# Two 256-token blocks per PSUM bank and eviction, HGRN products on VectorE, norm factors ahead of weight splits

## Chip, core and metric

One core of one Trainium2 chip runs the whole program. The metric is the device time of one execution in microseconds (us); lower is better.

## What is computed

Sequence 256, model width 1024, float32 in and out. A first block (a mixer of four branches, then a SwiGLU feed-forward, then a norm) is followed by a second block of two layers: an HGRN2 mixer and a feed-forward, an RG-LRU mixer and a feed-forward, and a last norm. Cut to what the change touches:

```python
# HGRN2, 8 heads of 128: S_t = diag(f_t) S_{t-1} + (1-f_t) i_t^T, o_t = S_t^T q_t
q, fl, v, g = split(rmsnorm(x, norm_mix_2[0]) @ hgrn_w_in)      # 4 x 1024 columns
lb = cumsum(softmax(hgrn_lb, axis=0), axis=0)[0]                # the floor of f
q = silu(q); f = lb + (1 - lb) * sigmoid(fl); k = (1 - lb) * sigmoid(-fl)
o = rmsnorm_per_head(recurrence(q, k, f, v)) * hgrn_norm * silu(g)
x = x + o @ hgrn_w_out
# RG-LRU
y, u = split(rmsnorm(x, norm_mix_2[1]) @ lru_w_in)              # 2 x 1024 columns
uc = causal_conv4(u); r = sigmoid(uc @ wa + ba); i = sigmoid(uc @ wx + bx)
a = exp(-8 * r * softplus(-lam)); b = sqrt(1 - a*a) * (i * uc)
x = x + (linear_scan(a, b) * gelu(y)) @ lru_w_out
```

## The kernel before

Every float32 product is made of three matmuls on split operands: `hh`, `hl` are the high and low part of the normed input, `whi`, `wlo` those of a weight. A weight unit `raw` (1 MB) comes by DMA on SP's queue into one of four buffers and is split in two halves of 128x1024: `whi` is a copy on ACT, `wlo` a subtraction on DVE (`split`, L99 and L100; with `burst` set, four of them on POOL). There are four buffers of each half.

Two forms of projection exist. `gemm_a` gives tokens on partitions, matmuls of 512 columns. `gemm_b` gives features on partitions: a block of 128 features by 256 tokens, eight k steps of three 256-column matmuls, 24 matmuls (`block_b`, L153 to L155). The pool of accumulators `acc` has four PSUM banks, one for each block. An eviction multiplies the block by `rrow`, the row of the norm's factors 1/rms, which `make_row` makes on PE from two diagonal tiles `dg` and ACT copies (L265); so matmuls may start before the factor is known, evictions may not. The factor itself is `rstd`: a sum, a scaling (L235, L241) and a power on POOL (L245).

Users of `gemm_b`: the first mixer's convolution inputs (`xin`) and query/key blocks (`qk`), HGRN's q and f blocks (`u`, L778 and L785), the LRU's convolution inputs (`xin`, L929) and its y blocks (`yg`, L977). In HGRN, POOL multiplies `hq = u * sigmoid(u)` (L781), makes the pair products `pr` and their low part `pl` (L833, L835), and scales the residual `x` by the factor `rf` of the first block's last norm (L1098). HGRN's scores are then built in seven levels (`tp` tiles of L864, with `hq`, `hk` multiplied by `G` in between, L868, L869, and `st` filled by L871), with HGRN's v and g projections (`acc`, 512 columns) as PE work between the levels. Each head group ends in an out chain: state products `tp<-hv,st` (L894), squares (L899, ACT), a factor (L241, L245), two multiplications to `on` (L902, L904), PE transposes of `on` (L273), a split into `oh` and `ol`, the output projection.

Instructions of each engine run in the order that a scheduler wrote at build time, by dependencies and priorities; weight splits have priority offset 400.

Of the kernel before, what the change touches and what calls it, by code (L numbers as in the profile page):

```python
# [74 lines left out]
class Build:  # L75
    def __init__(self, tc, a):
        self.tc, self.nc, self.a = tc, tc.nc, a
        self.uid = 0
        self.turn = 0
        self.share = 0  # L80
        self.parts = 2
        self.hold = []
        self.burst = 0
        self.wmore = None
        self.place = -1

# [144 lines left out]
    def rstd(self, ss, scale=1.0 / D):  # L231
# [3 lines left out]
        nc.vector.tensor_tensor(r, ss[:, :, 0], ss[:, :, 1], op=ALU.add)  # L235
        self.rsqrt(r, r, scale)
# [20 lines left out]
    def make_row(self, r):  # L257
        nc = self.nc
# [113 lines left out]
    def mixer(self, hk, r, rr, x, finish):  # L372
        nc, a, tc = self.nc, self.a, self.tc
        w_in = a["w_in"][0]
        with tc.tile_pool(name="yT", bufs=3) as ytp, tc.tile_pool(name="att", bufs=1) as at, \
# [136 lines left out]
            for ps in self.gemm_b(hk, w_in, 5136, 1):  # L512
                nc.vector.tensor_tensor(kd, ps, rr(), op=ALU.mult)
# [54 lines left out]

    def lru_rates(self):
# [21 lines left out]
    def conv_inputs(self, pool, n):  # L591

        xins = [pool.tile([P, S + 3], F32, name=self.nm("xin")) for _ in range(n)]
        for xin in xins:
            self.nc.vector.memset(xin[:, 0:3], 0.0)
        return xins
# [8 lines left out]
    def mamba(self, hk, r, rr, w_in, mp, rows4, dtc, acol, yT, then):  # L605
# [4 lines left out]
        xins = self.conv_inputs(mp, 2)  # L610
        for b in (4, 6, 0, 2):
            for j, ps in enumerate(self.gemm_b(hk, w_in, 512 + b * P, 2)):
                blk = b + j
                xin = xins[j]
                nc.vector.tensor_tensor(xin[:, 3:], ps, rr(), op=ALU.mult)
# [131 lines left out]
    def hgrn(self, hk, r, rr, x, finish):  # L747
# [3 lines left out]
        w = a["hgrn_w_in_2"][0]  # L751
        LV = (64, 32, 16, 8, 4, 2, 1)
        with tc.tile_pool(name="hgrn", bufs=1) as hp:
            lbp = self.col["hgrn_lb_2"]
            lb = hp.tile([P, 8], F32, name="lb")
            om = hp.tile([P, 8], F32, name="om")
            lt = hp.tile([P, 2, 8], F32, name="lt")
            nc.vector.tensor_tensor(lb, lbp[:, 0:8], lbp[:, 8:16], op=ALU.max)
            for i in range(2):
                nc.vector.tensor_tensor(lt[:, i], lbp[:, i * 8:(i + 1) * 8], lb, op=ALU.subtract)  # L760
            nc.scalar.activation(lt, lt, AF.Exp)
            nc.vector.tensor_tensor(om, lt[:, 0], lt[:, 1], op=ALU.add)
            nc.vector.reciprocal(om, om)
            nc.vector.tensor_tensor(lb, lt[:, 0], om, op=ALU.mult)
            nc.vector.tensor_tensor(om, lt[:, 1], om, op=ALU.mult)
# [58 lines left out]
    def hgrn_scores(self, hp, q, k, f, masks, LV):  # L824
# [83 lines left out]
    def lru(self, hk, r, rr, x, finish):  # L908
        nc, a, tc = self.nc, self.a, self.tc
        w = a["lru_w_in_2"][0]  # L910
        with tc.tile_pool(name="lru", bufs=1) as lp:
# [10 lines left out]
            xins = self.conv_inputs(lp, 4)  # L922

            def conv(n):
                g, m = divmod(n, 2)
                for i, ps in enumerate(self.gemm_b(hk, w, D + n * 256, 2)):
                    b = 2 * n + i
                    xin = xins[b % 4]
                    nc.vector.tensor_tensor(xin[:, 3:], ps, rr(), op=ALU.mult)  # L929
                    self.conv4(uc[g][:, 2 * m + i], xin, [cw[:, k * 8 + b:k * 8 + b + 1] for k in range(4)],  # L930
# [228 lines left out]
```

## Time and profile before

| | |
|---|---|
| median of 3 runs | 1181.28 us (1181.03 to 1183.28) |
| the profiled execution | 1183.03 us, of which 1181.3 us span and 1.7 us around it |
| PE / DVE / ACT / POOL busy | 96% / 62% / 52% / 7% of the span |
| mean granted TensorE clock | 0.987 |

A row of a timeline gives start, duration, engine, source line, operation, output<-inputs, shapes, count, and in brackets the engine's idle time before it and what ended that.

### The profile page before, as it was taken

The numbers are of one execution on the slowest core, as the hardware profiler recorded it, in microseconds if no ns is written. First come the engines' busy times: TensorE is split into PE (matmuls) and PEld (weight loads), VectorE is DVE, ScalarE is ACT, GpSimd is POOL, SyncE is SP. The second block draws the span as 40 slices with busy tenths as digits, with TensorE's granted clock in tenths as the row PEclk, the third lists the DMA queues.
The fourth block names the chain that finished last, engine by engine and source line by source line (L and its number), as shares of the span: only waits on it lengthen the run. The fifth ranks groups of instructions, "written<-read, shape, count | busy, mean of one in ns | idle before, by whom it ended". The sixth has DMA issues, their size and how long they took to land.

```text
span 1181.3 us, 15772 instructions
## 1 busy us (share of the span) xinstructions
PE 1139.4 (96%) x6308; PEld 980.3 (83%) x6308; DVE 737.3 (62%) x971; ACT 615.4 (52%) x908; POOL 82.9 (7%) x87
## 2 busy tenths in 40 slices
PE   7999999999999999998999999999998789999997
PEld 7899897888888888888989878888888778888886
DVE  7876655565575555456998575555556776555552
ACT  7655656754555445346543465444446775445441
POOL 1100010000000000007510140000000000000000
PEclk9999999999999999999999999999998889999999
DMA  9795345455556555555443347555554546555540
GB/s 298 192 283 169 87 156 181 149 178 180 202 178 195 190 178 179 184 180 171 142 145 108 106 143 250 181 183 168 200 159 147 175 126 203 188 178 178 163 159 36
DMA packets 120761, 202.78 MB, mean 172 GB/s; under 512 B 4244, under 2 KB 44437, under 8 KB 120688
## 3 DMA queue, kind: packets, MB, share of 16 engines
q1 hardware_dynamic: 117264, 192.59, 49.8%
q0 software_dynamic: 2992, 8.56, 2.6%
q8 instruction: 49, 0.80, 0.3%
q10 hardware_dynamic: 432, 0.63, 0.2%
q14 instruction: 24, 0.20, 0.0%
HBM read 200.64 MB, written 4.25 MB: 173 GB/s over the span
## 4 chain that ended last, share of the span: by engine, by line
PE 86%; DVE 6%; ACT 4%; DMA 3%; issue 2%; POOLq 0%; POOL 0%; ACTq 0%; DVEq 0%
PE acc L154 26%; PE acc L155 26%; PE acc L153 26%; DVE wlo L100 2%; DMA raw<-in_w_in_dram 2%; PE tp L273 2%; PE tp L864 2%; PE tp L694 1%; ACT whi L99 1%; PE tp L207 1%; PE tp L723 1%; DVE uc L603 0%; PE tp L731 0%; DMA rows<-acd 0%; DVE G L875 0%
## 5 line engine op out<-in xcount | busy, mean ns | idle before, releaser
L100 DVE TENSOR_TENSOR wlo<-raw,whi 128x1024 fp32r<-128x1024 f32 (+3 forms) x364 | 442.2, 1220 | 310.0 <-ACT whi L99 303.3
L99 ACT CAST whi<-raw 128x1024 fp32r<-128x1024 f32 (+3 forms) x372 | 382.1, 1033 | 365.4 <-PE acc L155 299.7
L155 PE MATMUL acc<-whi,hl 128*128 128x512 f32 (+2 forms) x832 | 316.3, 381 | 0.0
L154 PE MATMUL acc<-wlo,hh 128*128 128x512 f32 (+2 forms) x832 | 313.6, 377 | 1.3 <-DVE wlo L100 1.3
L153 PE MATMUL acc<-whi,hh 128*128 128x512 f32 (+2 forms) x832 | 311.3, 378 | 1.4 <-ACT whi L99 1.1
L154 PEld LDWEIGHTS acc<-wlo,hh 128*128 128x128 f32 x832 | 156.4, 188 | 31.1 <-DVE wlo L100 2.4
L153 PEld LDWEIGHTS acc<-whi,hh 128*128 128x128 f32 x832 | 156.3, 188 | 28.7 <-ACT whi L99 2.0
L155 PEld LDWEIGHTS acc<-whi,hl 128*128 128x128 f32 x832 | 156.4, 188 | 28.1 <-issue 0.7
L153 PE MATMUL acc<-hh,whi 128*128 128x256 f32 (+1 forms) x496 | 140.2, 285 | 5.7 <-DVE u L778 2.7
L155 PE MATMUL acc<-hh,wlo 128*128 128x256 f32 (+1 forms) x496 | 140.0, 284 | 1.4 <-DVE wlo L100 1.4
L154 PE MATMUL acc<-hl,whi 128*128 128x256 f32 (+1 forms) x496 | 140.2, 284 | 0.4 <-DVE hl L100 0.4
L154 PE MATMUL acc<-wlo,ah 128*128 128x512 f32 x264 | 103.1, 391 | 0.0
L155 PE MATMUL acc<-whi,al 128*128 128x512 f32 x264 | 102.6, 389 | 0.0
L153 PE MATMUL acc<-whi,ah 128*128 128x512 f32 x264 | 102.5, 390 | 0.0
L153 PEld LDWEIGHTS acc<-hh,whi 128*128 128x128 f32 (+1 forms) x496 | 93.5, 190 | 8.6 <-ACT whi L99 3.6
L155 PEld LDWEIGHTS acc<-hh,wlo 128*128 128x128 f32 (+1 forms) x496 | 93.7, 189 | 2.4 <-DVE wlo L100 2.2
L154 PEld LDWEIGHTS acc<-hl,whi 128*128 128x128 f32 (+1 forms) x496 | 94.1, 190 | 1.4 <-DVE hl L100 0.6
L155 PEld LDWEIGHTS acc<-whi,al 128*128 128x128 f32 x264 | 49.6, 188 | 10.2
L153 PEld LDWEIGHTS acc<-whi,ah 128*128 128x128 f32 x264 | 49.5, 188 | 10.2
L154 PEld LDWEIGHTS acc<-wlo,ah 128*128 128x128 f32 x264 | 49.6, 188 | 10.0
L99 ACT CAST ah<-tp 128x512 fp32r<-128x512 f32 (+1 forms) x36 | 19.8, 551 | 34.0 <-PE tp L273 34.0
L329 ACT ACTIVATE sg<-acc,rstd 128x512 f32<-128x512 f32 (+1 forms) x36 | 23.3, 648 | 20.4 <-PE acc L155 20.4
(306 smaller groups left out, 1260.0 us busy)
## 6 DMA issues: line engine op xcount, KB each, us to landing
raw<-in_ffn_w_in_dram SPq DMA_DIRECT2D x44, 1024.0 KB, 5.2
raw<-in_w_in_dram SPq DMA_DIRECT2D x33, 1024.0 KB, 5.2
raw<-in_ffn_w_out_dram SPq DMA_DIRECT2D x20, 1024.0 KB, 5.1
raw<-in_hgrn_w_in_dram SPq DMA_DIRECT2D x16, 1024.0 KB, 5.4
raw<-in_w_ffn_gate_dram SPq DMA_DIRECT2D x11, 1024.0 KB, 5.1
raw<-in_w_ffn_up_dram SPq DMA_DIRECT2D x11, 1024.0 KB, 5.1
raw<-in_w_ffn_down_dram SPq DMA_DIRECT2D x10, 1024.0 KB, 5.1
raw<-in_w_branch_dram SPq DMA_DIRECT2D x8, 1024.0 KB, 5.1
```

Source lines behind the costliest of these rows:

```text
L99: self.nc.scalar.copy(hi, src)
L100: (eng or self.nc.vector).tensor_tensor(lo, src, hi.bitcast(F32), op=ALU.subtract)
L153: mm(ps, sh, mh, start=start, stop=False)
L154: mm(ps, sh, ml, start=False, stop=False)
L155: mm(ps, sl, mh, start=False, stop=stop)
L207: last = nc.tensor.transpose(ps[:, j * P:(j + 1) * P], xc[:, j * P:(j + 1) * P], self.ident)
L273: nc.tensor.transpose(ps[:, j * P:(j + 1) * P], src[:, j * P:(j + 1) * P], self.ident)
L329: nc.scalar.activation(sg[:, :n], psg[t][:, :n], AF.Silu, scale=r[:, t:t + 1])
L694: nc.tensor.matmul(ps[par][:, jj * W:(jj + 1) * W], qT[pr, 2 * gi + jj, qt * P:(qt + 1) * P], kT(2 * gi + jj)[pr, :W], start=True, stop=True)
L723: nc.tensor.transpose(ps[:, i * P:(i + 1) * P], sp[:, i, b * P:(b + 1) * P], self.ident)
L864: nc.tensor.matmul(ps[:, c:c + 64], k[:, h, ts], q[:, h, ts].rearrange("p (n u l) -> p n u l", u=2, l=L)[:, :, 1], start=True, stop=True)
```

## The change

`gemm_b` puts the two blocks of a pair into the two halves of one bank, with k outermost and the blocks inside it, and hands back one 128x2x256 view; `times_row` evicts it in one instruction. The four banks hold four pairs. Users are rewritten to pairs (`xin`, `qk`, `u`, `sgq`, `yg`; `u` has two buffers of a pair, `sgq` one). HGRN's `hq`, `pr` and `pl` are made on DVE, its `x*rf` on ACT. The floors `lb`, `om` are made by a function called beside the first feed-forward (the scheduler puts them in front of the program's first matmuls). `rstd`, the row and the chain of `rf` get priority offset 600.

```diff
     def gemm_b(self, hk, w, c0, nblk):
         wk = self.wunit(w, 0, 8, c0, nblk * P)
-        return [self.block_b(hk, wk, slice(b * P, (b + 1) * P)) for b in range(nblk)]
+        ps = self.acc()
+        n, mm = len(hk), self.nc.tensor.matmul
+        with self.held():
+            for k, (h, l) in enumerate(hk):
+                for b in range(nblk):
+                    o, (wh, wl) = ps[:, b * S:(b + 1) * S], (u[:, b * P:(b + 1) * P] for u in wk[k])
+                    mm(o, wh, h, start=k == 0 and b == 0, stop=False, skip_group_check=True)
+                    mm(o, wh, l, start=False, stop=False, skip_group_check=True)
+                    mm(o, wl, h, start=False, stop=k == n - 1, skip_group_check=True)
+        return ps[:, :nblk * S].rearrange("p (b s) -> p b s", s=S)
+
+    def times_row(self, out, ps, rr):
+        self.nc.vector.tensor_tensor(out, ps, rr.unsqueeze(1).to_broadcast([P, ps.shape[1], S]), op=ALU.mult)
...
         r = self.small.tile([P, 2], F32, tag="rstd", name=self.nm("rstd"))
-        nc.vector.tensor_tensor(r, ss[:, :, 0], ss[:, :, 1], op=ALU.add)
-        self.rsqrt(r, r, scale)
+        with self.tc.high_priority(offset=self.rush):
+            nc.vector.tensor_tensor(r, ss[:, :, 0], ss[:, :, 1], op=ALU.add)
+            self.rsqrt(r, r, scale)
...
-                    for i, ps in enumerate(self.gemm_b(hk, w, h0 * P, 2)):
-                        u = hp.tile([P, S], F32, tag="u", name=self.nm("u"), bufs=3)
-                        nc.vector.tensor_tensor(u, ps, rr(), op=ALU.mult)
-                        sg = hp.tile([P, S], F32, tag="sgq", name=self.nm("sgq"), bufs=2)
-                        nc.scalar.activation(sg, u, AF.Sigmoid)
-                        nc.gpsimd.tensor_tensor(q[:, 2 * c + i], u, sg, op=ALU.mult)
...
+                    u = hp.tile([P, 2, S], F32, tag="u", name=self.nm("u"), bufs=2)
+                    self.times_row(u, ps, rr())
+                    sg = hp.tile([P, 2, S], F32, tag="sgq", name=self.nm("sgq"), bufs=1)
+                    nc.scalar.activation(sg, u, AF.Sigmoid)
+                    nc.vector.tensor_tensor(q[:, hs], u, sg, op=ALU.mult)
...
+            for t in range(2):
+                nc.scalar.activation(x[:, t], x[:, t], AF.Copy, scale=rf[:, t:t + 1])
...
-        nc.gpsimd.tensor_tensor(pr, q.rearrange("p h t -> p (h t)"), k.rearrange("p h t -> p (h t)"), op=ALU.mult)
-        nc.scalar.copy(ph, pr)
-        nc.gpsimd.tensor_tensor(pl, pr, ph.bitcast(F32), op=ALU.subtract)
+        nc.vector.tensor_tensor(pr, q.rearrange("p h t -> p (h t)"), k.rearrange("p h t -> p (h t)"), op=ALU.mult)
+        self.split(ph, pl, pr)
...
-            for t in range(2):
-                nc.gpsimd.tensor_scalar(x[:, t], x[:, t], rf[:, t:t + 1], None, op0=ALU.mult)
```

Source lines shift: of the lines above, the evictions are L202 after, `split` L100 and L101, the matmuls of pairs L195 to L197, the row L282 to L285, the transposes of `on` L293, the state products L919, `x*rf` L816.

The first place is the start of HGRN on DVE. Before, the floors stand between the factor's steps (L1090 to L1093 are `rstd`, L762 to L765 the floors), and each block has its own eviction:

```order
L1091 TENSOR_TENSOR rstd_4717<-rstd_4717,rf_4720 128x2
L762 TENSOR_TENSOR om<-lt 128x8
L1092 TENSOR_SCALAR rstd_4717<-rstd_4717 128x2
L763 RECIPROCAL om<-om 128x8
L1093 TENSOR_TENSOR rstd_4717<-rstd_4717,rf 128x2
L764 TENSOR_TENSOR lb<-lt,om 128x8
L765 TENSOR_TENSOR om<-lt,om 128x8
L100 TENSOR_TENSOR wlo_4982<-raw_4979,whi_4981 128x1024
L262 TENSOR_SCALAR dg_4820<-ident,rstd_4717 128x128
L262 TENSOR_SCALAR dg_4823<-ident,rstd_4717 128x128
L100 TENSOR_TENSOR wlo_4986<-raw_4979,whi_4985 128x1024
L778 TENSOR_TENSOR u_4818<-acc_4768,rrow_4826 128x256
```

The same place on DVE in the changed program:

```order
L1116 TENSOR_TENSOR rstd_4702<-rstd_4702,rf_4705 128x2
L1117 TENSOR_SCALAR rstd_4702<-rstd_4702 128x2
L1118 TENSOR_TENSOR rstd_4702<-rstd_4702,rf 128x2
L282 TENSOR_SCALAR dg_4791<-ident,rstd_4702 128x128
L282 TENSOR_SCALAR dg_4794<-ident,rstd_4702 128x128
L101 TENSOR_TENSOR wlo_4937<-raw_4934,whi_4936 128x1024
L202 TENSOR_TENSOR u_4789<-acc_4740,rrow_4797 128x512
L202 TENSOR_TENSOR u_4862<-acc_4813,rrow_4797 128x512
L101 TENSOR_TENSOR wlo_4941<-raw_4934,whi_4940 128x1024
L101 TENSOR_TENSOR wlo_5007<-raw_5004,whi_5006 128x1024
L805 TENSOR_TENSOR hq_4727<-u_4789,sgq_4800 128x512
```

The floors and a weight split are gone from in front of `dg`; the evictions are pairs; `hq` has joined the queue. On ACT the same stretch now has the residual's scaling ahead of a weight half and of the row:

```order
L1101 ACTIVATE junk_4697,ss_3278<-x 128x512
L816 ACTIVATE x<-x,rf 128x1024 x2
L100 CAST whi_4936<-raw_4934 128x1024
L285 COPY rrow_4797<-tp_4790 128x256
L100 CAST whi_4940<-raw_4934 128x1024
```

Before, an exponential with its table load stood there, and POOL held the scaling.

The second place is HGRN's first out chain on PE. Before, the last score products (L880), the state products (L894) and the transposes of `on` (L273) have 24 matmuls of HGRN's last projection between the last two (12 for `acc_5872` and 12 for `acc_5873`, of which the first and the last rows):

```order
L880 MATMUL tp_5597<-hq_5051,hk_5052 128x128 x4
L894 MATMUL tp_5750<-hv,st_5366 128x128 x4
L153 MATMUL acc_5872<-whi_5910,hh_3296 128x512
L154 MATMUL acc_5872<-wlo_5911,hh_3296 128x512
...
L154 MATMUL acc_5873<-wlo_5915,hh_3296 128x512
L155 MATMUL acc_5873<-whi_5914,hl_3298 128x512
L273 MATMUL tp_5766<-ident,on_5763 128x128 x4
```

In the changed program that projection is finished earlier, and PE has:

```order
L889 MATMUL tp_5508<-hq_5001,hk_5002 128x64 x8
L155 MATMUL acc_5803<-wlo_5845,hh_3270 128x512
L156 MATMUL acc_5803<-whi_5844,hl_3272 128x512
L905 MATMUL tp_5520<-hq_4727,hk_4728 128x128 x4
L905 MATMUL tp_5527<-hq_5001,hk_5002 128x128 x4
L919 MATMUL tp_5680<-hv,st_5296 128x128 x4
L293 MATMUL tp_5696<-ident,on_5693 128x128 x4
```

Nothing stands between the state products and the transposes any more; 43 matmuls of the v and g projections have moved ahead of the score levels.

The third place is the start of the LRU on DVE. Before, four blocks are evicted one behind the other, ahead of the convolution taps (L603):

```order
L100 TENSOR_TENSOR wlo_7917<-raw_7910,whi_7916 128x1024
L929 TENSOR_TENSOR xin_7605<-acc_7623,rrow_7680 128x256
L929 TENSOR_TENSOR xin_7606<-acc_7648,rrow_7680 128x256
L929 TENSOR_TENSOR xin_7607<-acc_7706,rrow_7680 128x256
L929 TENSOR_TENSOR xin_7608<-acc_7731,rrow_7680 128x256
L603 SCALAR_TENSOR_TENSOR uc_7597<-xin_7605,pcol,uc_7597 128x256 x2
```

The same place after:

```order
L101 TENSOR_TENSOR wlo_7928<-raw_7921,whi_7927 128x1024
L202 TENSOR_TENSOR xin_7535<-acc_7549,rrow_7605 128x2x256
L101 TENSOR_TENSOR wlo_7837<-raw_7830,whi_7836 128x1024
L636 SCALAR_TENSOR_TENSOR uc_7527<-xin_7535,pcol,uc_7527 128x256 x2
L202 TENSOR_TENSOR xin_7536<-acc_7630,rrow_7605 128x2x256
```

Taps now start behind the first pair, and PE's order has the second half of three pairs (`acc_7549`, `acc_7630`, then `acc_7702` of the y blocks, 23 matmuls each) one behind the other, where before the four `xin` blocks were finished first and 48 matmuls of y blocks followed.

## Rows read from the trace of the kernel before

**Rows 1.** The page: busy time of two engines, and the shares of the chain that ended last.

```profile
PE 1139.4 (96%) x6308; PEld 980.3 (83%) x6308; DVE 737.3 (62%) x971; ACT 615.4 (52%) x908; POOL 82.9 (7%) x87
PE 86%; DVE 6%; ACT 4%; DMA 3%; issue 2%; POOLq 0%; POOL 0%; ACTq 0%; DVEq 0%
```

**Rows 2.** The view of waits, PE: what it waited for, us in total, times, longest.

```profile
PE acc L153 <- ACT uh L99: 6.7, 2, 4.4
PE acc L153 <- ACT loh L99: 5.9, 1, 5.9
...
PE acc L153 <- DVE u L778: 2.7, 1, 2.7
PE tp L653 <- DVE mt L651: 1.6, 1, 1.6
PE acc L155 <- DVE wlo L100: 1.4, 2, 1.1
...
PE acc L155 <- DVE ol L104: 1.1, 2, 0.7
...
PE acc L154 <- DVE hl L100: 0.4, 1, 0.4
...
PE acc L153 <- DVE xin L615: 0.3, 1, 0.3
```

**Rows 3.** Windows of PE alone: stretch, its length, PE busy (and matmuls), granted clock, DMA share, GB/s. The first follows the wait for `u`, the second the wait for `loh`, the third is a feed-forward.

```profile
552.90:560.00 7.10, 7.08 (x47) 0.76 0.47 148
962.80:968.00 5.20, 5.14 (x15) 0.64 0.46 133
700.00:860.00 160.00, 160.00 (x777) 1.00 0.59 194
```

**Rows 4.** PE's timeline: a 512-column matmul that waited for a weight half.

```profile
603.64 0.50 PE L154 MATMUL acc<-wlo,hh 128*128 128x512 f32 x1 [0.75 <-DVE wlo L100]
```

**Rows 5.** A window of HGRN from the first eviction to the end of the first score level: length, then busy us and instructions of PE, weight loads, DVE, ACT, POOL, then clock.

```profile
552.40:612.20 59.80, 56.91 (x388) 52.27 (x388) 53.11 (x76) 29.95 (x47) 28.84 (x28) 0.97 0.45 142
```

**Rows 6.** DVE's instructions of the same window by line: count, busy us, mean ns, idle before.

```profile
L100 DVE TENSOR_TENSOR wlo<-raw,whi 128x1024 fp32r<-128x1024 f32 x17 | 24.5, 1441 | 3.5 <-ACT whi L99 3.4
L875 DVE TENSOR_TENSOR G<-hf 128x512 f32<-128x512 f32 x2 | 4.8, 2389 | 0.0
L778 DVE TENSOR_TENSOR u<-acc,rrow 128x256 f32<-128x256 f32 x8 | 3.2, 413 | 1.2 <-PE acc L155 1.2
L844 DVE TENSOR_TENSOR hq<-hq,hf 128x1024 f32<-128x1024 f32 x2 | 2.4, 1210 | 0.0
L868 DVE TENSOR_TENSOR hq<-hq,hf 128x512 f32<-128x512 f32 x2 | 1.4, 686 | 0.0
```

**Rows 7.** Timelines of DVE and POOL: three DVE instructions with two inputs in SBUF, and the POOL instruction beside each.

```profile
569.31 2.69 DVE L875 TENSOR_TENSOR G<-hf 128x512 f32<-128x512 f32 x1
574.51 2.39 DVE L875 TENSOR_TENSOR G<-G 128x32 f32<-128x32 f32 x1
600.16 3.43 DVE L100 TENSOR_TENSOR wlo<-raw,whi 128x1024 fp32r<-128x1024 f32 x1
...
569.04 2.40 POOL L833 TENSOR_TENSOR pr<-hq,hk 128x1024 f32<-128x1024 f32 x1 [3.67 <-DVE hk L790]
573.68 3.17 POOL L835 TENSOR_TENSOR pl<-pr,ph 128x1024 fp32r<-128x1024 f32 x1 [1.09 <-ACT ph L834]
600.07 2.44 POOL L835 TENSOR_TENSOR pl<-pr,ph 128x1024 fp32r<-128x1024 f32 x1 [1.17 <-ACT ph L834]
```

**Rows 8.** HGRN's first out chain, timelines of PE and DVE (the rows left out between the second and the third are 23 matmuls like the second).

```profile
656.55 1.06 PE L894 MATMUL tp<-hv,st 128*128 128x128 f32 x8
657.36 0.48 PE L153 MATMUL acc<-whi,hh 128*128 128x512 f32 x1
...
662.94 0.60 PE L273 MATMUL tp<-ident,on 128*128 128x128 f32 x4
...
665.40 0.50 PE L153 MATMUL acc<-whi,oh 128*128 128x512 f32 x1
...
660.87 0.69 DVE L904 TENSOR_TENSOR on<-on,hg 128x512 f32<-128x512 f32 x1
```

**Rows 9.** The row, the first evictions of `u` and the residual's factor at HGRN's start, timelines of ACT, DVE and POOL; the last is an ACT instruction of the LRU with the scaling's shape.

```profile
550.34 0.37 ACT L265 COPY rrow<-tp 128x256 f32<-128x256 f32 x1
...
552.46 0.74 DVE L778 TENSOR_TENSOR u<-acc,rrow 128x256 f32<-128x256 f32 x2
...
548.21 1.54 POOL L245 TENSOR_TENSOR rf<-rf,mhalf 128x2 f32<-128x2 f32 x1
...
952.03 1.04 ACT L961 ACTIVATE hs<-av 128x1024 f32<-128x1024 f32 x1
```

**Rows 10.** The first mixer's wait for `mt`, timeline of ACT: a weight half that waits for its DMA, and the table load behind it.

```profile
68.28 1.05 ACT L99 CAST whi<-raw 128x1024 fp32r<-128x1024 f32 x1 [6.04 <-DMA raw<-in_w_in_dram]
69.35 1.28 ACT L650 ACT_TABLE_LOAD   x1
```

**Rows 11.** The LRU's start, timelines of DVE and PE.

```profile
895.79 1.41 DVE L929 TENSOR_TENSOR xin<-acc,rrow 128x256 f32<-128x256 f32 x4
...
902.05 0.28 PE L155 MATMUL acc<-hh,wlo 128*128 128x256 f32 x1
904.59 0.83 PE L153 MATMUL acc<-uh,whi 128*128 128x256 f32 x4 [2.26 <-ACT uh L99]
```

More of the change, by code (lines that the diff above doesn't have):

```diff
@@ L85, in __init__ @@
         self.place = -1
+        self.rush = 600
     def nm(self, s):
@@ L257, in make_row, with row_of @@
     def make_row(self, r):
+        with self.tc.high_priority(offset=self.rush):
+            return self.row_of(r)
+    def row_of(self, r):
         nc = self.nc
@@ L567, in mixer, with hgrn_floors @@
             gp.__exit__(None, None, None)
+    def hgrn_floors(self):
+        nc = self.nc
+        self.floors = lb, om = [self.const.tile([P, 8], F32, name=n) for n in ("lb", "om")]
+        lbp = self.col["hgrn_lb_2"]
+        lt = self.small.tile([P, 2, 8], F32, tag="lt", name="lt", bufs=1)
+        nc.vector.tensor_tensor(lb, lbp[:, 0:8], lbp[:, 8:16], op=ALU.max)
+        for i in range(2):
+            nc.vector.tensor_tensor(lt[:, i], lbp[:, i * 8:(i + 1) * 8], lb, op=ALU.subtract)
+        nc.scalar.activation(lt, lt, AF.Exp)
+        nc.vector.tensor_tensor(om, lt[:, 0], lt[:, 1], op=ALU.add)
+        nc.vector.reciprocal(om, om)
+        nc.vector.tensor_tensor(lb, lt[:, 0], om, op=ALU.mult)
+        nc.vector.tensor_tensor(om, lt[:, 1], om, op=ALU.mult)
     def lru_rates(self):
@@ L591, in conv_inputs @@
     def conv_inputs(self, pool, n):
-        xins = [pool.tile([P, S + 3], F32, name=self.nm("xin")) for _ in range(n)]
+        xins = [pool.tile([P, 2, S + 3], F32, name=self.nm("xin")) for _ in range(n)]
         for xin in xins:
-            self.nc.vector.memset(xin[:, 0:3], 0.0)
+            self.nc.vector.memset(xin[:, :, 0:3], 0.0)
         return xins
@@ L609, in mamba @@
         bcT = mp.tile([P, 4, S], F32, name="bcT")
-        xins = self.conv_inputs(mp, 2)
+        xins = self.conv_inputs(mp, 1)
         for b in (4, 6, 0, 2):
-            for j, ps in enumerate(self.gemm_b(hk, w_in, 512 + b * P, 2)):
+            xin2 = xins[0]
+            self.times_row(xin2[:, :, 3:], self.gemm_b(hk, w_in, 512 + b * P, 2), rr())
+            for j in range(2):
                 blk = b + j
-                xin = xins[j]
-                nc.vector.tensor_tensor(xin[:, 3:], ps, rr(), op=ALU.mult)
+                xin = xin2[:, j]
                 cv = mp.tile([P, S], F32, tag="cv", name=self.nm("cv"), bufs=2)
@@ L744, in attention, with hgrn @@
             self.to_T(y[:, t], yT[0], yT[1], t)
-    def hgrn(self, hk, r, rr, x, finish):
+    def hgrn(self, hk, r, rr, rf, x, finish):
         nc, a, tc = self.nc, self.a, self.tc
         w = a["hgrn_w_in_2"][0]
+        lb, om = self.floors
         LV = (64, 32, 16, 8, 4, 2, 1)
         with tc.tile_pool(name="hgrn", bufs=1) as hp:
[L754 to L765, printed above, removed]
             v = hp.tile([P, 2, D], F32, name="hv")
@@ L920, in lru @@
                           for nm in ("rg", "ig", "av"))
[L922 removed]
+            xins = self.conv_inputs(lp, 2)
             def conv(n):
                 g, m = divmod(n, 2)
[L926 removed]
+                xin2 = xins[n % 2]
+                self.times_row(xin2[:, :, 3:], self.gemm_b(hk, w, D + n * 256, 2), rr())
+                for i in range(2):
                     b = 2 * n + i
[L928 to L930 removed]
+                    self.conv4(uc[g][:, 2 * m + i], xin2[:, i], [cw[:, k * 8 + b:k * 8 + b + 1] for k in range(4)],
                                cb[:, b:b + 1])
```

50 lines of the change are left out of this document (25 added, 25 removed).

## The prediction

> **What bounds the kernel now.** The page comes first: PE is busy 96% of the span and is 86% of the chain that ended last; DVE has 6% of it, ACT 4% [rows 1]. A window over a feed-forward has PE busy for all of its 160 us [rows 3], so nothing that only shortens DVE or ACT can pay there. What can be won or lost is PE's idle time, and the view of waits gives it by what ended it [rows 2]: in HGRN the wait for the first `u` (2.7), for two low weight halves (1.4), and at its start for `hl` (0.4); in the LRU `uh` (6.7) and `loh` (5.9); in the first mixer `mt` (1.6). Third come the windows that follow a long wait: after the wait for `u` the granted clock is 0.76 over 7.10 us, after that for `loh` 0.64 over 5.20 us, between the levels 1.2 and 2.4 GHz [rows 3]. So a wait costs more than itself: (1 - 0.76) x 7.10 = 1.7 us and (1 - 0.64) x 5.20 = 1.9 us behind these two.
>
> **HGRN, what goes.** Before, two pairs fill four banks, PE stops at the third pair, and `u` must be evicted first. With a pair to a bank, the third and fourth pair have banks of their own, 96 matmuls more, some 11 us at 0.115 each (half the columns, so half of the 0.23 that is read below), and the factors come about as they did. The wait (2.7) and the clock behind it (1.7) go. At HGRN's start PE has the first half of three pairs to do before it needs the last parts of the input, so the 0.4 for `hl` goes as well. Later waits for low weight halves, 1.4 [rows 2] and 0.75 [rows 4], follow DVE instructions that were stretched beside POOL's products (below); I let them go. Sum: 2.7 + 1.7 + 0.4 + 1.4 + 0.75 = 7.0 us less.
>
> **HGRN, what comes.** The order shows that v and g are projected earlier, so the first out chain loses its cover. Before, the state products end at 656.55 + 1.06 = 657.61 and the second multiplication to `on` ends at 660.87 + 0.69 = 661.56 [rows 8]: squares, factor and multiplications take 3.95 us, in which PE did 24 matmuls of the projection (657.36 to 662.94, 0.23 us each). After, transposes stand right behind the state products, and PE waits all 3.95 us. The clock then falls, as it did after 2.7 us; I price that like the stretch after `loh`, 1.9, of which about 0.7 is covered by the wait for `ol` that stands there now (1.1 in two, of which 0.7 here [rows 2]): 1.2. Together 5.1 us more.
>
> **DVE in between.** It is busy 53.1 of 59.8 us in this window [rows 5]; three things change it. It takes four `hq` of 128x512 at 0.69, two `pr` and two `pl` of 128x1024 at 1.21 [rows 6]: 4 x 0.69 + 4 x 1.21 = 7.6 us. Sixteen evictions of 0.41 [rows 6] become eight of 128x512 for which I take 0.69, the multiplication of that shape in [rows 8]: 6.6 - 5.5 = 1.1 less. And instructions get shorter that stand beside POOL's work: seventeen `wlo` have a mean of 1.44, where two products of that shape take 1.21; two `G` of 128x512 take 2.39 each, where others take 0.69 [rows 6]; one `G` of 32 columns takes 2.39 [rows 7], at least 1.7 too many. 17 x 0.23 + 2 x 1.70 + 1.7 = 9.0 less. So 53.1 + 7.6 - 1.1 - 9.0 = 50.6 us of work remain. PE, rid of its 7.0 us, asks for it in 59.8 - 7.0 = 52.8 us; the 43 matmuls put in before the levels give it 43 x 0.23 = 9.9 us more, with four more `wlo` and two gates (4 x 1.21 + 2 x 0.69 = 6.2) to do: 62.7 us for 56.8 of work. DVE can follow on the whole, with single waits where `hq`, `pr` or `pl` stand ahead of a weight half. Below, nothing; above, no stretch goes, 65.8 us of work face 62.7, and the first eviction comes some 0.9 later (next part): 4.0. I take 1.0, nearer the lower end because the stretch lies beside POOL's products in the rows that follow. HGRN: -7.0 + 5.1 + 1.0 = -0.9 us.
>
> The rows show what the stretch is: `G` of 569.31 ends at 572.00, 0.56 after POOL's `pr` ended (571.44); the `wlo` of 600.16 ends 1.08 after POOL's `pl` (602.51); the small `G` of 574.51 ends with `pl` at 576.9 [rows 7]. The Trainium skill says it as a rule ("SBUF — State Buffer", section "Who interferes with whom"): a VectorE instruction with two SBUF inputs and a GpSimd instruction that reads SBUF take turns at a shared port, whole instructions at a time. By that rule, the three rows agree, all of the stretch beside these products vanishes, and the sum would have 0 where I have 1.0 for new waits.
>
> **The residual's scaling on ACT.** Two instructions of 128x1024 at 1.04 [rows 9] now stand ahead of a `whi` and of the row, and wait for `rf`, which POOL has at 548.21 + 1.54 = 549.75. Scaling to 551.8, `whi` to 552.9, row to 553.3, against 550.34 + 0.37 = 550.71 before [rows 9]: 2.6 later (the first eviction began at 552.46, so it comes 0.9 later). Behind ACT's row DVE's pair evictions queue, and PE waits for their banks. But PE only needs a bank after four pairs: it stopped near 550.2 (2.7 before the first window of [rows 3]), and 11 us later is 561. So this costs nothing; without the cover of the third and fourth bank it would be 2.6.
>
> **LRU.** The first stall waits for convolution, on DVE. Before, four blocks are evicted from 895.79 in one run [rows 11]. After, the first pair's second half must be followed by 46 matmuls of the next two pairs until PE runs out (902.05 + 0.28 [rows 11]), 46 x 0.115 = 5.3, so the pair is whole at 897.0 and is evicted 1.3 us later, with less work behind it: in the whole LRU 16 evictions of 0.41 become eight of 0.69, 1.1 less, of which I count 0.5 on the path. Net +0.8; between -1.1 (the saving alone) and +2.6 (1.3 at both halves).
>
> **Mixer and start.** PE's wait for `mt` ends with an ACT exponential that stands behind a weight half waiting for its DMA and a table load [rows 10], and neither moves. PE has 117 instead of 125 matmuls of 256 columns before it, so the wait grows by 8 x 0.115 = 0.9; the wait for `xin`, 0.3 [rows 2], may go: +0.6, between -1.6 (the wait vanishes because the weight comes earlier) and +1.6. The floors' seven small DVE instructions (some 0.1 each) and an exponential now stand beside the first norm: +0.3, between 0 and 0.8; in HGRN they were off PE's path once the banks suffice. The rest of the priority change orders factors for feed-forwards, where PE has no wait; nothing.
>
> **Sum.** -0.9 + 0.8 + 0.6 + 0.3 = +0.8 against the profiled execution's 1183.03 us: 1183.8. That execution lies 1.75 above the median of the runs, so 1182.1. A measurement of this kernel tells about 0.2%, 2.4 us, from no change.
>
> **Rivals.**
> *The gain stays.* DVE's stretch goes entirely, no new wait, the LRU has the saving alone, the mixer is as before: -7.0 + 5.1 - 1.1 = -3.0; if the clock is not lost behind the chain, -4.2, and if `mt` comes earlier too, -5.8. For it: the rows on the stretch; against it: the uncovered chain, which takes most back in every case. With -4.2 it is 1183.03 - 4.2 - 1.75 = 1177.1.
> *DVE becomes HGRN's bound.* One place, DVE's queue from the first pair to the first score level: it is 53.1 of 59.8 busy. If the stretch belongs to something else than POOL's products (POOL keeps its masks), the new 7.6 us push weight halves past PE's demand, +4.0 instead of +1.0: 1182.1 + 3.0 = 1185.1. It decides once these waits reach 2.5 (1182.1 + 1.5 = 1183.6), which is 62.7 - 0.9 + 2.5 = 64.3 us of DVE work.
> *Nothing moves in HGRN,* since the row comes 2.6 later through ACT. Against it: free banks until 561. It would need the row past 560; with the wait and its clock back and 2.6 on top, 1182.1 + 2.7 + 1.7 + 2.6 = 1189.1, and I give it almost nothing.
>
> **How the numbers follow.** The balance has 0.45, and a range of its own from 1179 to 1184, the same bounds within one or two us; the gain that stays 0.26; DVE's bound, or the upper bounds of LRU and mixer together, 0.29. The range reaches to the outer cases' times and a little past them, 1176.7 to 1185.7. Faster by over 0.2% (below 1178.9) has 0.26, within 0.45, slower (above 1183.6) 0.29.
>
> **What would show it.** In the changed trace: no wait for `u` and no fallen clock near 553; one of about 4 us ahead of the first transposes of `on` (L293), with a lower clock behind it; `wlo` and `G` near 1.21 and 0.69 through HGRN, single waits for low halves under 1 us; the first wait for `uh` or `ul` about 1 us longer, that for `mt` about 0.9. I would be wrong if the chain's wait is missing, if waits for weight halves in HGRN add up to over 3 us, or if the LRU's stalls differ by more than 2 us.

## The result and the profile after

The changed kernel takes 1197.41 us (median of four runs, 1195.54 to 1199.09) where the kernel before took 1182.28 on the same chip: a ratio of 1.0121, 95% interval 1.0101 to 1.0141. It is slower by 15 us; the forecast was 1182.1, between 1176.7 and 1185.7. The profiled execution has a span of 1195.2 us against 1181.3.

The page after, as in [rows 1]:

```profile
PE 1153.6 (97%) x6308; PEld 990.2 (83%) x6308; DVE 729.7 (61%) x948; ACT 614.7 (51%) x897; POOL 55.0 (5%) x73
...
PE 87%; ACT 4%; DVE 3%; issue 3%; DMA 2%; POOL 0%; POOLq 0%; ACTq 0%; DVEq 0%
```

PE has as many matmuls as before (6308) and is busy 14.2 us longer with them. Its idle time hardly differs: 35.1 us before, 34.9 after, added up from the timeline. The view of waits (PE: us in total, times, longest) shows that it was exchanged:

```profile
PE tp L687 <- DVE mt L685: 6.7, 1, 6.7
PE tp L293 <- DVE on L929: 5.5, 2, 4.1
PE acc L154 <- ACT loh L100: 5.3, 1, 5.3
...
PE acc L154 <- DVE yg L202: 3.6, 1, 3.6
...
PE acc L154 <- ACT uh L100: 2.3, 2, 2.0
PE acc L155 <- DVE ul L101: 2.1, 1, 2.1
PE acc L155 <- DVE wlo L101: 0.5, 1, 0.5
```

Against [rows 2], the wait for `u` is gone and those for low weight halves fell; `on` came (5.5) and `mt` grew from 1.6 to 6.7. Windows of PE (length, busy and matmuls, granted clock): the stretch of the second feed-forward that answers to the third of [rows 3], the mixer around the wait for `mt`, HGRN before and behind its last score level.

```profile
710.60:870.60 160.00, 160.00 (x765) 1.00 0.59 194
70.00:80.00 10.00, 7.18 (x60) 1.00 1.01 338
80.00:90.00 10.00, 6.14 (x33) 0.66 0.70 225
540.00:655.00 115.00, 115.00 (x763) 1.00 0.51 164
655.00:690.00 35.00, 29.45 (x176) 0.95 0.18 60
```

The first line is the riddle. PE is busy for all of 160 us at clock 1.00, as before, in a stage whose code the change does not touch, and does 765 matmuls where it did 777.

The stages, measured on PE's timeline from first transpose to first transpose of `x` (the first mixer part ends at the transposes of `xs`), in us; the last four columns are kernels of the experiments:

| stage | before | after | pads_before | change_old_addresses | convs_as_before | change_mended |
|---|---|---|---|---|---|---|
| mixer, first part | 91.2 | 103.2 | 90.5 | 102.7 | 89.7 | 93.5 |
| mixer, rest | 253.4 | 252.5 | 255.4 | 248.9 | 256.2 | 252.2 |
| feed-forward 1 | 165.5 | 167.2 | 167.2 | 165.5 | 165.5 | 165.5 |
| HGRN | 177.7 | 175.6 | 177.2 | 174.2 | 173.9 | 173.6 |
| feed-forward 2 | 170.2 | 172.1 | 172.1 | 170.3 | 170.3 | 170.3 |
| LRU | 125.7 | 125.5 | 125.5 | 124.2 | 125.1 | 125.6 |
| feed-forward 3 | 190.8 | 192.5 | 192.5 | 190.8 | 190.8 | 190.8 |

Two losses, then: some 12 us in the mixer's first part, and 1.7 to 1.9 in each feed-forward. (Part of the 12 is work that changed sides: PE does 605 matmuls in the first part after, 581 before.)

### The profile page after: what moved, and what is told of

Same layout as the page of the kernel before. It is cut to its first block, busy times and chain, and to the rows that moved or that the text cites. A ratio compares the mean times of both kernels' runs of the same rounds, so it can differ in the third digit from the quotient of the medians.

```text
span 1195.2 us, 15682 instructions
## 1 busy us (share of the span) xinstructions
PE 1153.6 (97%) x6308; PEld 990.2 (83%) x6308; DVE 729.7 (61%) x948; ACT 614.7 (51%) x897; POOL 55.0 (5%) x73
## 4 chain that ended last, share of the span: by engine, by line
PE 87%; ACT 4%; DVE 3%; issue 3%; DMA 2%; POOL 0%; POOLq 0%; ACTq 0%; DVEq 0%
PE acc L155 23%; PE acc L154 23%; PE acc L156 23%; PE acc L195 3%; PE acc L196 3%; PE acc L197 3%; PE tp L293 2%; PE tp L889 2%; PE tp L728 1%; DMA rows<-acd 1%; DVE wlo L101 1%; ACT whi L100 1%; PE tp L222 1%; DVE uc L636 1%; PE tp L757 1%
## 5 line engine op out<-in xcount | busy, mean ns | idle before, releaser
L101 DVE TENSOR_TENSOR wlo<-raw,whi 128x1024 fp32r<-128x1024 f32 (+3 forms) x364 | 438.0, 1209 | 317.0 <-ACT whi L100 312.1
L100 ACT CAST whi<-raw 128x1024 fp32r<-128x1024 f32 (+3 forms) x372 | 381.9, 1032 | 388.3 <-PE acc L156 315.8
L155 PE MATMUL acc<-wlo,hh 128*128 128x512 f32 (+2 forms) x832 | 317.2, 381 | 0.5 <-DVE wlo L101 0.5
L197 PE MATMUL acc<-hh,wlo 128*128 128x256 f32 x456 | 130.2, 286 | 0.0
L196 PE MATMUL acc<-hl,whi 128*128 128x256 f32 x456 | 130.1, 286 | 0.0
L195 PE MATMUL acc<-hh,whi 128*128 128x256 f32 x456 | 129.5, 286 | 0.0
L196 PEld LDWEIGHTS acc<-hl,whi 128*128 128x128 f32 x456 | 86.8, 190 | 0.6 <-issue 0.3
L195 PEld LDWEIGHTS acc<-hh,whi 128*128 128x128 f32 x456 | 86.7, 191 | 0.7 <-issue 0.3
L197 PEld LDWEIGHTS acc<-hh,wlo 128*128 128x128 f32 x456 | 86.8, 190 | 0.1
L100 ACT CAST ah<-tp 128x512 fp32r<-128x512 f32 (+1 forms) x36 | 19.9, 552 | 34.7 <-PE tp L293 34.7
```

The source lines that it names most:

```text
L100: self.nc.scalar.copy(hi, src)
L101: (eng or self.nc.vector).tensor_tensor(lo, src, hi.bitcast(F32), op=ALU.subtract)
L155: mm(ps, sh, ml, start=False, stop=False)
L195: mm(o, wh, h, start=k == 0 and b == 0, stop=False, skip_group_check=True)
L196: mm(o, wh, l, start=False, stop=False, skip_group_check=True)
L197: mm(o, wl, h, start=False, stop=k == n - 1, skip_group_check=True)
```

## Experiments

**Addresses.** The change adds tiles for the floors to two pools that lie ahead of the operands: `lb` and `om` (32 bytes a partition each) to the constants, `lt` (64) to the small tiles. `x`, `hh` and `hl` thereby move by 64 bytes, the weight tiles and all behind them by 128. `pads_before` gives the kernel before idle tiles of these sizes:

```
+    for n in ("pad0", "pad1"):
+        self.nc.vector.memset(self.const.tile([P, 8], F32, name=n), 0.0)
+    self.nc.vector.memset(self.small.tile([P, 2, 8], F32, tag="pad2", ...), 0.0)
```

> The kernel before with three idle tiles of the sizes that the floors' tiles have after the change (two of 32 bytes per partition in the pool of constants, one of 64 in the pool of small tiles), each cleared once; every instruction and its order on each engine stay as before, and only the addresses move, to those of the changed kernel: x, hh and hl by 64 bytes, raw, whi, wlo and what lies behind them by 128. Theory A (the changed kernel's matmuls run slower because of where their operands lie): the 512-column matmuls of gate and up go from 229 ns apart to 232 to 233, the 256-column ones from about 116 to 119, and the kernel takes 8 to 12 us more, 1190 to 1194 us. Theory B (the pace comes from the new order of work or from what runs beside it): no change, 1182 +- 2 us. The first mixer stage should look as before in both (1.6 us wait for mt near 70 us).

Measured: 1192.25 us against 1182.95, ratio 1.0071 (1.0055 to 1.0086). The same 160 us of the second feed-forward:

```profile
702.40:862.40 160.00, 160.00 (x764) 1.00 0.59 194
```

Nothing but three idle tiles, and 764 matmuls where there were 777, every feed-forward as long as in the changed kernel, the mixer's first part about as before. Theory A holds for the pace. `floors_behind` goes the other way:

```
-self.const.tile([P, 8], F32, name=n)          # lb, om; lt likewise
+self.fl.tile([P, 8], F32, name=n)             # a pool behind the weight tiles
```

> The changed kernel with the three tiles of the floors (lb, om, lt) in a pool of their own behind the weight tiles, so that x, hh, hl, raw, whi and wlo lie where they lay in the kernel before; instructions and orders are those of the changed kernel. Theory A (addresses): the pace of before comes back (229 and 116 ns) and the kernel takes 8 to 12 us less than the changed one, 1185 to 1189 us; what is left over the kernel before is the mixer's wait. Theory B (order or neighbours): as the changed kernel, 1197 +- 2 us. In both the 6.7 us wait for mt near 77 us stays.

Measured: 1192.24 us, ratio 1.0073 (1.0059 to 1.0088): 5 less than the changed kernel, not 8 to 12. Gate, up and the 256-column matmuls got their pace back, but the new pool pushed `ah` and `al` by 128 bytes against the weights, and the down projections lost theirs. The mean distance between the starts of neighbouring matmuls at full clock (from the timeline, in ns), beside the distance of the operands' addresses modulo 256 (activations less weights, from the builds):

| kernel | `hh` − `whi` | gate, up (512) | 256 columns | `ah` − `whi` | down (512) |
|---|---|---|---|---|---|
| before | 192 | 229.2 | 115.8 | 0 | 226.9 |
| pads_before | 128 | 232.7 | 118.7 | 0 | 226.9 |
| after | 128 | 232.7 | 119.0 | 0 | 226.9 |
| floors_behind | 192 mostly | 230.0 | 115.5 | 128 mostly | 231.2 |
| change_old_addresses | 192 | 229.2 | 116.3 | 0 | 226.9 |
| before_aligned | 0 | 227.6 | 119.8 | 0 | 226.9 |

The down projections moved by 128 bytes together with their weights in `after` and kept 226.9; it is the distance that counts, not the place. `pace_by_offset` measures this by itself:

```
+for n, d in enumerate((0, 0, 32, 64, ..., 1024)):      # bytes
+    h = st[:, d // 4 + j * 128:][:, :128]; wh = mv[:, j * 512:][:, :512]
+    # 48 x (h, wh), (h, wl), (l, wh) into one bank; then the same with 256 columns
```

> Not the computation, only its matmuls: two tiles of SBUF filled once from x, and then TensorE alone in the kernel's pattern of three (high by high, high by low, low by high), no split, no DMA and no eviction beside it. 17 blocks of 144 matmuls with 512 moving columns, then 17 with 256, each block with the operand tile (the stationary one in the first half, the moving one in the second) shifted further against the weight tile: by 0, 0, 32, 64, 96, 128, 160, 192, 224, 256, 288, 320, 384, 448, 512, 768 and 1024 bytes. Theory A (the pace follows the distance of the two operands' addresses modulo 256, whatever runs beside it): 512 columns 227 ns apart at 0, 256, 512, 768 and 1024, 229 at 192 and 448 (and 64, 320), 232 to 233 at 128 and 384; 256 columns 114 to 116 at 0 and 64, 119 at 128. Rival (the distance matters only against what the other engines and the DMA read and write): every block at the same pace within 0.5 ns. The output is not the reference's.

DVE's timeline there has one small copy at the end of each block of 144 matmuls. The rows that end blocks 96, 128, 160, 192, 224 and 256 with 512 columns, then those that end 0, 0, 96, 128, 160 and 192 with 256 columns:

```profile
178.27 0.17 DVE L1058 COPY xo<-acc 128x8 f32<-128x8 f32 x1 [33.55 <-PE acc L1057]
211.73 0.17 DVE L1058 COPY xo<-acc 128x8 f32<-128x8 f32 x1 [33.29 <-PE acc L1057]
245.33 0.17 DVE L1058 COPY xo<-acc 128x8 f32<-128x8 f32 x1 [33.44 <-PE acc L1057]
278.31 0.17 DVE L1058 COPY xo<-acc 128x8 f32<-128x8 f32 x1 [32.81 <-PE acc L1057]
311.90 0.17 DVE L1058 COPY xo<-acc 128x8 f32<-128x8 f32 x1 [33.43 <-PE acc L1057]
344.55 0.17 DVE L1058 COPY xo<-acc 128x8 f32<-128x8 f32 x1 [32.48 <-PE acc L1057]
...
593.36 0.17 DVE L1058 COPY xo<-acc 128x8 f32<-128x8 f32 x1 [17.11 <-PE acc L1057]
610.64 0.17 DVE L1058 COPY xo<-acc 128x8 f32<-128x8 f32 x1 [17.11 <-PE acc L1057]
...
661.84 0.17 DVE L1058 COPY xo<-acc 128x8 f32<-128x8 f32 x1 [17.10 <-PE acc L1057]
678.92 0.17 DVE L1058 COPY xo<-acc 128x8 f32<-128x8 f32 x1 [16.92 <-PE acc L1057]
695.82 0.17 DVE L1058 COPY xo<-acc 128x8 f32<-128x8 f32 x1 [16.73 <-PE acc L1057]
712.15 0.17 DVE L1058 COPY xo<-acc 128x8 f32<-128x8 f32 x1 [16.16 <-PE acc L1057]
```

Differences by 144: with 512 columns 234.2 ns at 96 (from the copy before it, at 144.55), 232.4 at 128, 233.3 at 160, 229.0 at 192, 233.3 at 224, 226.7 at 256, and 226.7 again at 512, 768 and 1024, 232.4 at 384, 229.0 at 448. The first blocks can't be read from the copies: they come 1.6, 1.1 and 0.7 us behind the next block's first matmul, all later ones 0.2, so their differences are some 3 ns a matmul too short. Windows of PE from a block's first matmul to the next one's (144 matmuls, and one more that is still under way), for blocks 32, 64 and 288:

```profile
77.17:110.74 33.57, 33.57 (x145) 1.00 0.00 0
110.74:144.34 33.60, 33.60 (x145) 1.00 0.00 0
344.34:377.93 33.59, 33.59 (x145) 1.00 0.00 0
```

That is 233.1, 233.3 and 233.3 ns (320, from its copy, 233.3). So with 512 columns theory A holds at every pair of distances that are equal modulo 256, with TensorE alone and in one execution; only the 229 expected at 64 and 320 was wrong. Two things differ with 256 columns. They go the other way: 120.0 at 0, 118.6 at 128, 113.4 at 192; 114 to 116 at 0 had been expected. And 448 takes 117.8 where 192 takes 113.4, so there 256 is not the whole period. (The shifted tile is the stationary operand with 512 columns and the moving one with 256. The kernels' own 256-column matmuls with `hh` stationary take 117.7 at 192 in `before` and 119.9 at 0 in `before_aligned`, so the order goes with the columns.) `before_aligned` pays for that:

```
+nc.vector.memset(self.small.tile([P, 48], F32, tag="pad", name="pad", bufs=1), 0.0)
```

> The kernel before with one idle tile of 192 bytes per partition in the pool of small tiles: raw, whi, wlo and all behind them move by 192, so hh and hl now lie at a multiple of 256 bytes from whi and wlo (192 before); no order changes. Theory A: gate and up go from 229 to 227 ns (2100 matmuls of 512 or 320 columns: about -5 us), those of 256 columns from 116 to 114 or 115 (1750 of them: -2 to -4 us), and the kernel takes 1174 to 1178 us. Rival (the distance of before was as good as any, or it is not the distance modulo 256): 1181 to 1185 us.

Measured: 1180.74 us, ratio 0.9989 (0.9979 to 0.9999). Gate and up got faster (229.2 to 227.6), the 256-column matmuls slower (115.8 to 119.8), and the forecast of 1174 to 1178 was missed by its second half. What is left of a gain comes from where these matmuls stand: the feed-forwards, where PE never waits, take all of a faster pace (0.5 to 0.7 us each), while in the mixer, HGRN and the LRU a slower one partly only fills waits (for `uh` 5.6 us instead of 6.7). The profiled execution also lost less clock (mean granted clock 0.993 instead of 0.987), so the two paces alone do not give the 1.6 us.

**The change without its addresses.** `change_old_addresses` works out the floors in place:

```
-self.floors = lb, om = [self.const.tile(...) ...]; lt = self.small.tile(...)
+lt = self.col["hgrn_lb_2"].rearrange("p (a b) -> p a b", a=2); top = self.col["norm_mix"]
+self.floors = lt[:, 0], lt[:, 1]
```

> The changed kernel with the floors worked out in place in the parameter columns (lb and om over hgrn_lb_2's own 16 columns, the maximum in norm_mix's 8, which nothing reads any more by then), so that no tile is added and every tile from hh to al lies at its address of before. TensorE's order is the changed kernel's, row by row; DVE and ScalarE place the floors' ten small instructions a little later. What is left over before is the change without its addresses: the mixer's wait (about +6 to 7 us with the half clock) less what HGRN gains (3 to 4 us). Theory A: 1185 to 1189 us, with gate and up at 229, the down projections at 227 and 256 columns at 116 ns. If the addresses explained everything, 1182; if nothing, 1197.

Measured: 1185.62 us, ratio 1.0021 (1.0009 to 1.0032). So 11.8 of the 15.1 us are addresses, and its stage column gives the rest: mixer +7.0, HGRN −3.5, LRU −1.5. The wait for `mt` is there in full:

```profile
PE tp L688 <- DVE mt L686: 8.0, 1, 8.0
```

**The wait for mt.** The changed kernel's timelines of POOL, DVE and PE:

```profile
43.27 0.54 DVE L417 COPY rv<-tp 8x383 f32<-8x383 f32 x1
45.69 0.51 POOL L418 DMA_DIRECT2D relv<-rv  x1 [9.64 <-DVE rv L417]
50.65 2.23 POOL L421 DMA_DIRECT2D skew<-relv  x2 [4.44 <-DMA relv<-rv]
71.91 0.81 POOL L468 DMA_DIRECT2D bias<-skew  x1 [19.03 <-DMA skew<-relv]
72.71 0.57 POOL L458 DMA_DIRECT2D rows<-acd  x1
...
81.19 0.35 DVE L682 TENSOR_SCALAR mt<-rows,tcol 128x256 f32<-128x256 f32 x1 [11.82 <-DMA rows<-acd]
...
83.86 0.69 PE L687 MATMUL tp<-xc,mt 128*128 128x64 f32 x2 [6.68 <-DVE mt L685]
```

and DVE's and POOL's of the kernel before:

```profile
35.03 0.54 DVE L397 COPY rv<-tp 8x383 f32<-8x383 f32 x1
37.45 0.52 POOL L398 DMA_DIRECT2D relv<-rv  x1 [3.82 <-DVE rv L397]
42.75 2.23 POOL L401 DMA_DIRECT2D skew<-relv  x2 [4.78 <-DMA relv<-rv]
63.21 0.82 POOL L448 DMA_DIRECT2D bias<-skew  x1 [18.23 <-DMA skew<-relv]
66.08 0.55 POOL L438 DMA_DIRECT2D rows<-acd  x1 [2.05 <-DVE mt L649]
```

The second `rows` transfer stands on POOL's queue behind that of the attention's bias, which waits for `skew`, the transfer that follows the one-hot products by way of `rv` and `relv`. Before, the bias went at 63.21, and `rows` then waited only for its buffer. After, `rv` is 8 us later, the bias goes at 71.91, and `rows`, whose buffer was read for the last time at 63.7, goes behind it at 72.71 and is there 8.5 us later. `bias_first` asks for the bias earlier:

```
+skew_bias()
-self.mamba(..., new_yT(), skew_bias)
+self.mamba(..., new_yT(), lambda: None)
```

> The changed kernel with the relative bias (one-hot products, relv, skew) asked for ahead of the mamba branch instead of behind its four convolution pairs; the build then places the two products after 155 rows of TensorE instead of 227 (179 in the kernel before). Theory C (the mt wait is the skew chain's: the second rows transfer stands on GpSimd's queue behind the bias transfer, which waits for skew, which came 8 us later because 48 more matmuls went ahead of the one-hot products): the bias transfer no longer waits, the mt wait of 6.7 us falls to under 2 us, the half clock behind it goes, and the kernel takes 5 to 8 us less, 1189 to 1192 us. Rival D (the rows transfer itself, 512 KB beside the weights, or the free mt buffers set the wait): the wait stays above 5 us, 1195 to 1198 us. The pace of the matmuls stays slow in both.

Measured: 1187.69 us, ratio 1.0043 (1.0029 to 1.0057), 9.7 under the changed kernel where 5 to 8 were expected; the wait is 0.8 us. Theory C holds, with more to gain than was worked out. `both_mended` joins this to `floors_behind`:

> The two edits before together: floors' tiles behind the weight tiles, relative bias ahead of the mamba branch. If A and C hold, their sum: 13 to 18 us under the changed kernel, 1179 to 1184 us, so about the kernel before or a little under it. If only A holds, 1185 to 1189; if only C, 1189 to 1192; if neither, 1197.

Measured: 1184.94 us, ratio 1.0016 (1.0005 to 1.0027), just above the sum's range; the down projections' new distance (231.2 instead of 226.9 ns) is in it. Why `rv` came late is told by `convs_as_before`:

```
-self.times_row(xin2[:, :, 3:], self.gemm_b(hk, w_in, 512 + b * P, 2), rr())
+pair = [self.block_b(hk, wk, slice(j * P, (j + 1) * P)) for j in range(2)]
+nc.vector.tensor_tensor(xin[:, 3:], pair[j], rr(), op=ALU.mult)      # for each j
```

> The changed kernel at the addresses of before, and in the mamba branch alone the convolution pairs as they were: each 256-token block with an accumulator and an eviction of its own, two input tiles. The build puts the one-hot products back after 179 rows of TensorE (227 with shared banks). Theory E (it is the shared bank that let the last pair of 48 matmuls go ahead of the one-hot products, because a pair takes one accumulator of the four instead of two, and so made the skew chain and the second rows transfer late): the mt wait falls from 8 us to 1 to 2 us and the time from 1185.6 to 1177 to 1180 us. Rival (the wait has other causes, such as the attention's shared banks behind it): 1183 to 1186 us.

Measured: 1179.02 us, ratio 0.9966 (0.9953 to 0.9979), and the wait for `mt` at 1.9 us. Theory E holds: with two banks for each pair, PE had to wait for the fourth pair's (the 0.3 for `xin` in [rows 2]), and the build filled that place with the one-hot products. With one bank, the pair's 48 matmuls go first, and a chain that takes 28 us from `rv` to the bias starts 8 us later.

**HGRN.** `change_mended` has the old addresses and the early bias, and is the base of two more:

> The changed kernel with the floors in place in the parameter columns (hh, hl, whi, wlo, ah and al at their addresses of before: 192 bytes modulo 256 between hh and whi, 0 between ah and whi) and the relative bias asked for ahead of the mamba branch. Worked out from the runs: 1185.6 of the kernel with old addresses less the 7 to 9.5 us that the bias was worth at the other addresses: 1176 to 1178.5 us, 4 to 6 under the kernel before. By the block measurement (256 columns 113 to 118 ns at 192 against 120 at 0; 512 columns 229 against 227) it should be 2 to 4 us under the aligned version (1178.8). If the two distances weigh alike, 1178 to 1180.

Measured: 1179.24 us, ratio 0.9969 (0.9960 to 0.9978). With the distance 0 instead of 192 it is `change_aligned`:

> The changed kernel with the floors in place in the parameter columns, the relative bias asked for ahead of the mamba branch, and the idle tile of 192 bytes that sets hh and hl at a multiple of 256 bytes from whi and wlo. Theory A and C: HGRN's gain stays, the mixer's wait is gone, and the pace is faster than before's: 1170 to 1175 us, 8 to 13 us under the kernel before. If the distance modulo 256 is not it: 1179 to 1183 us.

Measured: 1178.8 us, ratio 0.9966 (0.9954 to 0.9979). The two distances weigh alike after all (1178 to 1180, the last case above), and the forecasts of 1176 to 1178.5 and of 1170 to 1175 were 0.7 and 3.8 us too low, as that of `before_aligned` had been. `mended_no_rush` sets `self.rush = 0`:

> The mended kernel (floors in place, bias first) with the norm factors at their ordinary priority, as before the change. Prediction's step: in HGRN the 2.7 us wait for u and the half clock behind it come back: 3 to 5 us more, all of it at HGRN's start, 1180 to 1183 us. Rival: the products' leaving GpSimd and the joint evictions had already ended that wait: no difference, within 1 us.

Measured: 1177.14 us, ratio 0.9959 (0.9944 to 0.9973). No wait for `u` came back (HGRN 173.8 us against 173.6): the priority of the norm factors did nothing for HGRN. That the whole is 2.1 us below `change_mended` is not clear of the scatter of the two. The first `u` is evicted 16.4 us behind the first of HGRN's 256-column matmuls, no earlier than before (16.2), and by then PE has begun 134 of them, where the four banks of before hold 96: the shared banks ended that wait. `mended_products_on_gpsimd` moves the products back:

```
-nc.vector.tensor_tensor(q[:, hs], u, sg, op=ALU.mult)      # and pr, pl, x by rf
+nc.gpsimd.tensor_tensor(q[:, hs], u, sg, op=ALU.mult)
```

> The mended kernel with HGRN's products (u by sigmoid, q by k, the difference for its low part) and the scaling of x back on GpSimd, two 256-token blocks at a time. Prediction's step: the wlo splits and G products beside GpSimd are stretched again, single waits for wlo of 0.3 to 1.1 us come back (1.4 us in all) and the chain behind x4 products gets later: 1 to 3 us more, 1178 to 1181 us; the 4.1 us wait for on at HGRN's end may shrink, since the scores come later anyway. Rival: GpSimd's lateness costs as much as it gives: no difference within 1 us.

Measured: 1178.33 us, ratio 0.9967 (0.9955 to 0.9979): no difference, but another trace, and again no wait for `u`. PE's waits, and then two groups of DVE's lines in 60 us of HGRN (count, busy us, mean ns):

```profile
PE acc L155 <- DVE wlo L101: 3.3, 3, 2.0
...
PE acc L197 <- DVE wlo L101: 1.5, 2, 0.8
```

```profile
L101 DVE TENSOR_TENSOR wlo<-raw,whi 128x1024 fp32r<-128x1024 f32 x18 | 23.8, 1332 | 3.8 <-ACT whi L100 3.8
...
L902 DVE TENSOR_TENSOR G<-G 128x64 f32<-128x64 f32 x2 | 4.8, 2420 | 0.0
```

and the answering groups of the changed kernel:

```profile
L101 DVE TENSOR_TENSOR wlo<-raw,whi 128x1024 fp32r<-128x1024 f32 x21 | 25.4, 1221 | 5.3 <-ACT whi L100 5.2
...
L900 DVE TENSOR_TENSOR G<-G 128x64 f32<-128x64 f32 x2 | 0.4, 218 | 0.0
```

The stretched instructions and the waits for low halves come back (4.8 us, of which 0.5 stand in the mixer in every version), and the wait for `on` (4.9 in `change_mended`) is not in the list at all: the build leaves 24 matmuls of a projection to cover the out chain. HGRN takes 174.7 instead of 173.6.

## Why the prediction was wrong, step by step

**The pace of PE: the step that failed, and 11.8 us.** The whole working prices a matmul at 0.23 or 0.115 us before and after, and counts the floors as "seven small DVE instructions": +0.3. What they cost was their tiles' 128 bytes. Every matmul of 512 columns on `hh` became 3.5 ns longer and every one of 256 about 3.2: 2112 x 3.5 + 1755 x 3.2 = 13.0 us (counts from the build), of which 11.8 reached the time (9.3 in `pads_before`, where some of it filled waits: `uh` 5.9 us instead of 6.7). [rows 3] gave the reason to look: a stage with PE busy for all of its 160 us depends on nothing but the pace, so an unchanged stage is not an argument that nothing happens there. The build lists the addresses.

**Mixer: +0.6 forecast, +7.0 measured at equal addresses.** "PE's wait for `mt` ends with an ACT exponential …, and neither moves" took the last releaser in [rows 10] for the only one. What it missed is POOL's queue: the row transfer behind the bias, whose chain begins with two products on PE. So the wait came to 8.0 us, 6.4 more, where 0.9 more was forecast, and the clock fell (0.66 from 80 to 90 us in the changed kernel). The order of PE showed these products move by 48 rows. That the wait for `xin` "may go" was right; its going is what let the 48 matmuls ahead.

**HGRN: −0.9 forecast, −3.5 measured at equal addresses.** The wait for `u` went, as did those for `hl`, for the low halves and the first for `ol`. The first out chain lost its cover as worked out: 4.1 us against 3.95. Wrong in size: a second wait for `on` of 1.4 was not seen, and new waits on DVE (+1.0) did not come, so the sum with 0 that the prediction gave beside its own was nearer. Waits were about as forecast in all (5.5 us instead of 6.7); the rest of the −3.5 is pace. By form, added up from PE's starts at the old addresses, the 256-column matmuls take 2.3 us less, those of 512 columns 1.4 less, transposes and products of 128 columns 1.6 more, for the low clock (0.95 over 35 us in the last window above, 1.75 us, about as priced) now falls on them, between the two waits for `on`. Some 0.5 of the 1.4 is an address again, an estimate from the builds and the table: `oh` and `ol` lie 128 bytes from `whi` in the kernel before and 0 in the changed one. Nor is the 1.7 for the clock behind `u` a fixed price: in `before_aligned` the same wait of 2.7 us is followed by full clock, where the first of [rows 3] has 0.76:

```profile
552.90:560.00 7.10, 7.10 (x59) 1.00 0.49 148
```

The step "the factors come about as they did" stands, and the priority was rightly given no gain; the expectation of `mended_no_rush` called that wait the prediction's step, but the prediction had put its end down to the banks.

**LRU: +0.8 forecast, −0.1 to −1.5 measured at the old addresses.** The first stall grew as said (`uh` and `ul` 3.6 to 4.1 us together), but only the first half of the stage was worked out; at the second stall `uh`, `yg` and `ul` went from 6.9 to 4.0, where fewer evictions had been put at 0.5. The stalls differ by 3.1 us in all (16.5 us of idle time before, 13.4 after), more than the 2 that the prediction named as a sign of being wrong. The −1.5 of `change_old_addresses` holds some luck: its stage has a granted clock of 0.93 instead of 0.92, and with 0.92 `change_mended` takes 125.6 us, as before.

**Feed-forwards: "nothing"** was right for the priority and the floors' work (165.5, 170.3 and 190.8 us with the old addresses) and wrong by 5.3 us as soon as the tiles moved. Without the addresses the stages add to +2 (the medians to +3) against a forecast of +0.8, but by errors of both signs. Of the rivals, none named either mechanism.

## What to carry to other kernels

A change that adds a tile moves every tile behind it: compare the addresses of the matmul operands between two builds before pricing anything, and read PE's pace as a number of its own, by matmuls in equal windows of a stage that the change leaves alone. And where more accumulators let matmuls run ahead, look for the short piece of work that they now pass, above all one that starts a chain of DMAs on an in-order queue: with the old addresses and that piece ahead again, the same change takes 0.3% off (`change_mended`, and `convs_as_before` with the mixer's convolution pairs as they were) instead of adding 1.2%.

## What was not expected of the hardware

TensorE's rate depends on the distance of its two operands' addresses in SBUF, with no other engine running: from 226.7 to 234.2 ns for 512 columns and from 113.4 to 120.0 for 256, best at multiples of 256 bytes for the first and at 192 for the second. What in the chip does it was not looked into; that 192 differs from 448 with 256 columns stays open.
